# Eight modulation units between the layers, and the experts' outputs scattered in token order

## The chip, the core and the metric

The kernel runs on one core of a Trainium2 chip. The metric is the device time of one execution in microseconds (us). TensorE is called PE (its weight loads PEld), VectorE DVE, ScalarE ACT, GpSimd POOL and SyncE SP; a name with a q at its end (SPq, ACTq) is that engine's sequencer issuing a DMA.

## The reference

Two layers of a diffusion transformer block work on 256 context tokens and 256 x tokens of width 1024. All arithmetic is float32.

```python
mod = split(silu_c @ w_ada[l] + b_ada[l], 6)        # sh1, sc1, g1, sh2, sc2, g2; the same for ctx with silu_cc
hx = rms_norm(x, norm1_g[l]) * (1 + sc1) + sh1      # hc likewise
mix_x, mix_c = token_mixers(hx, hc, w_in[l], ...)   # differential, grouped and window attention
x = x + g1 * (mix_x @ w_out[l])
hx = rms_norm(x, norm2_g[l]) * (1 + sc2) + sh2
x = x + g2 * moe_ffn(hx, ...)                       # ctx too, except in the last layer
```

`moe_ffn` gives each token two of 16 experts (the best two of the best group of four); an expert computes `(silu(t @ w_gate) * (t @ w_up)) @ w_down` with 256 hidden columns, and the token's output is the sum of its two experts' outputs by their gates. The last layer updates x alone, and a final rms norm ends the program.

## The kernel before

Names in this section are those of the kernel's code; "layer one" is `l == 0`.

**Weights** pass through a ring of buffers (`Ring`), 1 MB each. `queue` writes down all loads of the program in the order in which they will be used. `load` takes the first of that list whenever a buffer is free, and issues its DMA on SP's queue; `take` hands the oldest loaded buffer to a user, `give` returns it and loads the next. Each buffer belongs to a pool that lives up to some layer (`last`). Pools are opened as SBUF comes free: `rawA` lives throughout, `rawB` opens ahead of the output projection, and `rawC` opens after it, ahead of the experts (two buffers in layer one, three in layer two). `upto` holds back loads of a later layer.

**Products** of float32 are made of three passes: ACT rounds a weight tile to a high part (`whi`, L234), DVE or POOL subtracts it to get the low part (`wlo`, L235), and `mm3` (L205 to L207) multiplies high by high, low by high and high by low.

**Modulation** of a layer is three thirds of `w_ada`, each eight loads (`kc`) of 1 MB. A unit (L459) multiplies one load with the two condition vectors in four groups of 32 columns of PE, into the PSUM bank `ada`. After the eighth unit of a third, DVE adds the bias (L465), PE transposes the row, and small products follow. `ada_third` is a generator that yields after each unit; `STEPS` says how many yields a third has. `fill(n)` runs n steps of it. `FILL` says for each layer how many steps run in the input projection, in attention and in the output projection: 28 in layer one's attention, 19 in layer two's, which are 16 units and three finishing steps. In attention these are spread over the items (L968 on): one tick of the loop works at several stages of several items in an order written by hand, and ends with the tick's share of `fill`. Each pool set of PSUM (`PS_IN`, `PS_ATT`, `PS_OUT`) has one of eight banks for `ada`; `PS_MOE` has none.

**Layer one's experts** (`experts`, L1006) work on 512 tokens, with 128 slots for each expert. `Route` picks the experts, and `lists` makes the list `idx` of the tokens of each expert, and `rows`, the place of each token's two outputs. Ahead of that the 512 normalized tokens were stored to `h2row` in DRAM, tile by tile, on SP's queue (L1772). POOL gathers an expert's tokens from there with an indirect DMA (L1025); PE transposes them (`tokens`), makes the hidden layer (`first`, `hidden`), and transposes it (`turn`); `second` multiplies with `w_down`. `write` copies the two PSUM banks of the output to `y` on ACT and issues a plain DMA of 128 rows on ACT's queue to `yrows` (L1095). `produce` splits the next weights: POOL makes the low part of the second half of `w_down`, DVE all others. The work of all engines is in the order written, since the loop is under a manual schedule. In the loop `write(n - 2)` follows `turn(n - 1)`, and two loads are let through in the last round.

**Between the layers** (`next_in`, L760) `combine` has POOL gather each token's two rows of `yrows` with eight indirect DMAs, by `rows`. For each of four tiles, `sum_pairs` makes the sum: ACT scales the first by its gate (`one`, L1405), DVE adds the second times its gate (`both`, L1408), `times` multiplies with g2 (L1411; on DVE for the first tile, on POOL for the other three), and DVE adds to x (L1414). Interleaved with it, `tokens_in` takes each tile through the norm (L655 makes `xn`), PE's transposes, the modulation and the high and low parts, and PE starts layer two's first block of `w_in` tile by tile. g2 comes broadcast into a buffer of the ring (`load_g2`).

**Layer two's experts** serve 256 tokens in pairs of experts (`expert_pairs`). They stream 48 MB of weights. They scatter their outputs into `prow` with an indirect DMA of POOL.

## Time and profile before

| what | value |
|---|---|
| time, median of 3 runs | 888.96 us (886.82 to 890.14) |
| the profiled execution | 888.22 us |
| its span in the profile | 886.3 us |
| PE busy | 784.3 us, 88% |
| DVE busy | 582.4 us, 66% |
| ACT busy | 447.6 us, 50% |
| POOL busy | 222.2 us, 25% |
| moved by DMA | 219.18 MB, mean 247 GB/s |

An engine's busy share is a mean over stages with different limits; which wait ends last in a stage is read from the stretches, the timelines and the chain of waits, whose rows stand below. In a timeline row the brackets hold the idle time ahead of the instruction and what ended it.

### The profile page before, as it was taken

What the parts mean: (1) busy time and instruction counts of PE and PEld (TensorE: products, weight loads), DVE (VectorE), ACT (ScalarE), POOL (GpSimd) and SP (SyncE); (2) the same over time, 40 slices, a digit from 0 to 9 for tenths busy, and PEclk for the clock granted to TensorE, in tenths of its full rate; (3) what the DMA queues carried; (4) which work ended last, traced back from release to release, by engine and by line L of the source; (5) the groups of instructions that cost most, each with busy time, mean ns of one, the idle gap of its engine ahead of it and who ended that gap; (6) DMA issues with size and microseconds to landing.
All of it is one profiled execution on the core that took longest, in us unless ns stands there. A gap on an engine that the chain in (4) does not pass through costs nothing.

```text
span 886.3 us, 12972 instructions
## 1 busy us (share of the span) xinstructions
PE 784.3 (88%) x4731; PEld 576.3 (65%) x4731; DVE 582.4 (66%) x1200; ACT 447.6 (50%) x861; POOL 222.2 (25%) x258
## 2 busy tenths in 40 slices
PE   4899999889989977999999549998899797999984
PEld 0578878445557746999999438887555565656541
DVE  1577673879863798899999586697667566221226
ACT  2454442667773416888888546462466543111112
POOL 2000101556320133443342472100423101000200
PEclk9999999999999988999999859999899997999987
DMA  9952221667879337899993757342188955999981
GB/s 319 344 185 96 95 96 48 247 270 284 275 214 376 121 148 263 306 388 401 400 408 156 249 195 292 128 158 95 51 331 215 340 186 215 350 423 422 419 333 51
DMA packets 54505, 219.18 MB, mean 247 GB/s; under 512 B 10299, under 2 KB 10299, under 8 KB 36640
## 3 DMA queue, kind: packets, MB, share of 16 engines
q1 hardware_dynamic: 40816, 182.34, 55.0%
q0 software_dynamic: 8736, 24.92, 7.9%
q10 hardware_dynamic: 4880, 11.00, 3.2%
q8 instruction: 39, 0.64, 0.3%
q14 instruction: 34, 0.28, 0.1%
HBM read 207.09 MB, written 16.84 MB: 253 GB/s over the span
## 4 chain that ended last, share of the span: by engine, by line
PE 66%; DVE 16%; DMA 8%; ACT 3%; issue 3%; POOL 2%; SPq 0%; ACTq 0%; POOLq 0%; DVEq 0%
PE mm L207 7%; PE mm L206 7%; PE mm L205 7%; PE tp L193 6%; PE gu L1189 6%; PE ada L459 4%; PE gu L207 4%; PE gu L205 3%; PE gu L206 3%; DMA wraw<-in_w_up 3%; PE sc L1466 3%; PE w L1245 3%; DVE wlo L235 2%; PE w L1154 2%; DVE nm L1480 2%
## 5 line engine op out<-in xcount | busy, mean ns | idle before, releaser
L235 DVE TENSOR_TENSOR wlo<-wraw,whi 128x1024 fp32r<-128x1024 f32 x136 | 186.1, 1392 | 43.0 <-ACT whi L234 40.5
L234 ACT CAST whi<-wraw 128x1024 fp32r<-128x1024 f32 x152 | 152.8, 1050 | 57.7 <-PE mm L207 35.5
L205 PE MATMUL mm<-whi,Xh 128*128 128x512 f32 x288 | 116.3, 405 | 5.1 <-ACT Xh L690 4.7
L206 PE MATMUL mm<-wlo,Xh 128*128 128x512 f32 x288 | 115.3, 400 | 0.5 <-DVE wlo L235 0.5
L207 PE MATMUL mm<-whi,Xl 128*128 128x512 f32 x288 | 115.0, 399 | 0.5 <-DVE Xl L694 0.5
L221 POOL TENSOR_TENSOR rstd<-ms,cst 128x1 f32<-128x1 f32 (+2 forms) x34 | 29.4, 864 | 272.1 <-DVE ms L219 263.2
L1493 ACT ACTIVATE e<-sc,nm 128x512 f32<-128x512 f32 (+1 forms) x96 | 58.4, 613 | 42.4 <-DVE nm L1486 22.6
L207 PE MATMUL gu<-whi,xl 128*128 128x256 f32 x256 | 74.3, 290 | 0.0
L205 PE MATMUL gu<-whi,xh 128*128 128x256 f32 x256 | 74.2, 290 | 0.0
L206 PE MATMUL gu<-wlo,xh 128*128 128x256 f32 x256 | 72.7, 284 | 0.0
L1189 PE MATMUL gu<-wraw,xq 128*64 128x256 f32 x512 | 64.4, 396 | 3.7 <-DMA wraw<-in_w_up 3.7
L205 PEld LDWEIGHTS mm<-whi,Xh 128*128 128x128 f32 x288 | 55.1, 191 | 18.7 <-ACT Xh L690 6.2
L207 PEld LDWEIGHTS mm<-whi,Xl 128*128 128x128 f32 x288 | 55.0, 191 | 13.9 <-DVE Xl L694 1.5
L206 PEld LDWEIGHTS mm<-wlo,Xh 128*128 128x128 f32 x288 | 55.1, 191 | 12.8 <-DVE wlo L235 1.2
L235 POOL TENSOR_TENSOR wlo<-wraw,whi 128x1024 fp32r<-128x1024 f32 x16 | 42.7, 2672 | 81.1 <-ACT whi L234 50.3
L1189 PEld LDWEIGHTS gu<-wraw,xq 128*64 128x64 f32 x512 | 37.9, 142 | 24.1 <-DMA wraw<-in_w_up 4.2
L193 PEld LDWEIGHTS tp<-ident,e 128*128 128x128 f32 x240 | 26.1, 142 | 40.8 <-issue 21.1
L1480 DVE TENSOR_REDUCE nm<-sc 128x1 f32<-128x512 f32 x64 | 41.2, 684 | 16.5 <-PE sc L1466 11.6
L207 PEld LDWEIGHTS gu<-whi,xl 128*128 128x128 f32 x256 | 49.3, 193 | 1.1 <-DVE xl L1050 0.4
L205 PEld LDWEIGHTS gu<-whi,xh 128*128 128x128 f32 x256 | 49.6, 194 | 0.3 <-ACT xh L1049 0.3
L206 PEld LDWEIGHTS gu<-wlo,xh 128*128 128x128 f32 x256 | 49.5, 193 | 0.0
L193 PE MATMUL tp<-ident,e 128*128 128x128 f32 x240 | 37.8, 286 | 8.4 <-DVE e L1534 3.9
(348 smaller groups left out, 1625.4 us busy)
## 6 DMA issues: line engine op xcount, KB each, us to landing
wraw<-in_w_ada SPq DMA_DIRECT2D x40, 1024.0 KB, 4.9
wraw<-in_w_gate SPq DMA_DIRECT2D x32, 1024.0 KB, 10.1
wraw<-in_w_up SPq DMA_DIRECT2D x32, 1024.0 KB, 11.0
wraw<-in_w_down SPq DMA_DIRECT2D x32, 1024.0 KB, 14.1
wraw<-in_w_in SPq DMA_DIRECT2D x14, 1024.0 KB, 5.2
wraw<-in_w_ada SPq DMA_DIRECT2D x16, 512.0 KB, 8.1
yrows<-y ACTq DMA_DIRECT2D x16, 512.0 KB, 8.1
wraw<-in_w_in POOLq DMA_DIRECT2D x5, 1024.0 KB, 11.9
```

The costliest lines, as they stand in the source:

```text
L193: self.nc.tensor.transpose(out, in_, self.k["ident"][:n, :n])
L205: mm(out, lhsT=xh, rhs=wh, start=start, stop=False)
L206: mm(out, lhsT=xh, rhs=wl, start=False, stop=False)
L207: mm(out, lhsT=xl, rhs=wh, start=False, stop=stop)
L221: nc.gpsimd.tensor_tensor(r, ms, self.k["mhalf"][:, :width], OP.pow)
L234: nc.scalar.copy(h, raw[:, lo:hi])
L235: (engine or nc.vector).tensor_tensor(l, raw[:, lo:hi], h.bitcast(F32), OP.subtract)
L459: nc.tensor.matmul(ps[32 * j:32 * j + 32, :], lhsT=self.silu_c[:, kc, :], rhs=raw[:, 512 * j:512 * j + 512], start=kc == 0, stop=kc == NKC ...
L1189: nc.tensor.matmul(gu[PSLOTS * g:PSLOTS * g + PSLOTS, 256 * b:256 * b + 256], lhsT=xq[q][:, kc, c:c + PSLOTS], rhs=raw[:, kc * 256:kc * 25 ...
L1245: nc.tensor.matmul(y[hf][gs], lhsT=hT[:, c, 0:PSLOTS] if p == NP else hT[:, c, gs], rhs=raw[:, c * D + o * 512:c * D + o * 512 + 512], sta ...
L1480: V.reduce_max(self.nm[:, i:i + 1], self.ps[i], axis=AX.X)
L1493: nc.scalar.activation(self.e[i][:, :self.nkey], self.ps[i], AF.Exp, scale=0.125, bias=self.nm[:, i:i + 1], accum_out=self.z[i])
```

## The change

- `ada` gets a PSUM pool of its own, one bank, open from the start until layer two's experts; the other sets lose their `ada` bank.
- Eight of layer two's units (`GAP`, third 1, 8 MB of `w_ada`) are queued after layer one's expert weights, the next g2 and half of the first block of `w_in`; they may use only buffers of pools that end with layer one. PE runs them after the last `write` of layer one's experts (`fill(GAP)`). Layer two's attention then has 13 steps, eight of them units; layer one's has 31 steps, its units as before. Each third has one step more, since the addition of the bias became a step of its own.
- Layer one's `rawC` has four buffers in place of two. A free buffer is chosen by the least `last`, and a loaded one is taken by its name.
- The experts' outputs of layer one go to `orow`, whose rows stand in the order (token, first or second pick): POOL scatters an expert's rows there with an indirect DMA by a list `outs`, which leaves unused slots out. `idx` is `outs` shifted right by one; `rows` is no longer computed. The last expert but one is written ahead of the last.
- `combine` loads with eight plain DMAs, four on SP's queue and four on ACT's. All four `times` are on DVE, and the order of the steps in `next_in` is changed.

```diff
     0, 128, 256, 512, 640, 768, 784, 788, 796, 804, 820, 821, 837, 839)
-RAW = dict(A=4, D=2, B=(4, 3), C=(2, 3))
+RAW = dict(A=4, D=2, B=(4, 3), C=(4, 3, 2))
 WSP = dict(proj=4, out=(4, 4), moe=5)
-PS_IN = dict(mm=4, ada=1, tp=3)
-PS_ATT = dict(sc=3, ada=1, tp=2, poA=1, poB=1)
-PS_OUT = dict(mm=2, tp=2, rps=1, pps=1, ips=1, ada=1)
+PS_IN = dict(mm=4, tp=3)
+PS_ATT = dict(sc=3, tp=2, poA=1, poB=1)
+PS_OUT = dict(mm=2, tp=2, rps=1, pps=1, ips=1)
...
 CBS = (4, 2, 1, 0, 3)
-FILL = ((0, 28, 0), (0, 19, 0))
+FILL = ((0, 31, 0), (0, 13, 0))
+GAP = 8
...
         self.upto = 2
-    def add(self, key, src):
-        self.todo.append((key, src))
+    def add(self, key, src, layer=None, fits=None):
+        layer = key[1] if layer is None else layer
+        self.todo.append((key, src, layer, fits or (lambda last: last >= key[1])))
...
         for _ in range(min(n or len(self.todo), len(self.todo))):
-            if not n and self.todo[0][0][1] > self.upto:
+            key, src, layer, fits = self.todo[0]
+            if not n and layer > self.upto:
                 break
-            slot = next((s for s in self.free if s[2] >= self.todo[0][0][1]), None)
+            slot = min((s for s in self.free if fits(s[2])), key=lambda s: s[2], default=None)
...
                 break
-            key, src = self.todo.popleft()
+            self.todo.popleft()
...
             self.load()
-        k, slot, t = self.live.popleft()
-        assert k == key, (k, key)
-        return t, slot
+        unit = next(u for u in self.live if u[0] == key)
+        self.live.remove(unit)
+        return unit[2], unit[1]
...
             self.h2row = self.dram.tile([512, D], F32, name="h2row")
-            self.yrows = self.dram.tile([NEXP * SLOTS * max(self.npass), D], F32, name="yrows")
+            self.orow = self.dram.tile([1024, D], F32, name="orow")
...
             self.queue()
+            adap = tc.tile_pool(name="adap", bufs=1, space=PSUM, reuse_waits="tile")
+            self.adap, self.close_adap = adap.__enter__(), lambda: adap.__exit__(None, None, None)
...
         steps = deque((l, third, kc) for l in range(2) for third in range(1 - l, 3) for kc in range(self.STEPS[third]))
-        def ada(n):
+        def ada(n, *where):
...
                     ring.add(("ada", l, third, kc), a["w_ada"][l].rearrange("(p k) n -> p k n", k=NKC)[
-                        :, kc, third * 2048:third * 2048 + 2048])
+                        :, kc, third * 2048:third * 2048 + 2048], *where)
...
                 ring.add(("ada0", 0, h, q), w[:, 2 * q:2 * q + 2, 0:2, h, :])
-        def block(name, l, cb, n):
-            for h in range(2):
+        def block(name, l, cb, n, halves=(0, 1), *where):
+            for h in halves:
...
                 else:
-                    ring.add((name, l, cb, h), src.rearrange("(k p) n -> p k n", p=128))
+                    ring.add((name, l, cb, h), src.rearrange("(k p) n -> p k n", p=128), *where)
...
             for i, cb in enumerate(CBS):
-                block("w_in", l, cb, fw[2 * i:2 * i + 2])
+                block("w_in", l, cb, fw[2 * i:2 * i + 2], (1,) if l and not i else (0, 1))
...
                         ring.add(("w_down", l, q, f), a["w_down"][l, f].rearrange("(p k) n -> p k n", k=2))
-            ring.add(("g2", l + 1), lambda t, l=l: self.load_g2(l, t))
+            ring.add(("g2", l + 1), lambda t, l=l: self.load_g2(l, t), l)
+            if l == 0:
+                block("w_in", 1, CBS[0], (0, 0), (0,), 0)
+                ada(GAP, 0, lambda last: last == 0)
...
             nc.gpsimd.dma_start(self.n1g, a["norm1_g"][0].rearrange("(k p) -> p k", p=128))
-        ps = self.bank("ada")
+        ps = self.adap.tile([128, 512], F32, tag="ada", name="ada")
...
             dma(g, a["norm1_g"][l].rearrange("(k p) -> p k", p=128))
-        ps = self.bank("ada")
+        ps = self.adap.tile([128, 512], F32, tag="ada", name="ada")
...
             self.ring.give(slot)
-            if kc < NKC - 1:
-                yield
+            yield
...
         yield
-    STEPS = (9, 10, 9)
+    STEPS = (10, 11, 10)
...
         rc_cm, rc = opened("rawC", "left")
-        self.ring.open(rc, "rawC", RAW["C"][paired], l)
+        self.ring.open(rc, "rawC", RAW["C"][0 if l == 0 else 1 if paired else 2], l)
...
         self.wsp, self.nwsp = mo, WSP["moe"]
+        if l == 1:
+            self.close_adap()
...
                 self.experts(l, mo, route[0])
-                self.gates, self.rows = route[1:]
+                self.gates = route[1]
...
                     self.chunk(ps, [t], kc, parts)
-            for name, t in (("one", 0), ("both", 0), ("times", 0), ("one", 1), ("add", 0)):
+            for name, t in (("one", 0), ("one", 1), ("both", 0), ("times", 0), ("add", 0)):
...
             step(ins, 0, "root")
-            step(sums, 1, "times", self.nc.gpsimd)
...
                 step(ins, t - 1, "scale")
-                step(sums, t + 1, "both")
-                step(sums, t + 1, "times", self.nc.gpsimd)
-                step(sums, t, "add")
+                step(sums, t, "times")
...
                 step(ins, t - 1, "high", 1)
+                step(sums, t, "add")
...
                 step(ins, t, "root")
+                step(ins, t - 1, "low", 1)
+                step(sums, t + 1, "both")
...
                     self.ring.until(2, self.nc.gpsimd)
-                step(ins, t - 1, "low", 1)
...
             return route
-        return route.lists(), route.gates, route.rows
+        return route.lists(), route.gates
...
                 out=xg[n % 3], out_offset=None, in_=self.h2row[:, :],
-                in_offset=bass.IndirectOffsetOnAxis(ap=lists[ps][:, e:e + 1], axis=0),
+                in_offset=bass.IndirectOffsetOnAxis(ap=lists[ps][0][:, e:e + 1], axis=0),
...
                 self.copy(y[:, hf * 512:hf * 512 + 512], ys[n][hf], True)
-            r0 = (e * self.npass[l] + ps) * SLOTS
-            self.written = nc.scalar.dma_start(self.yrows[r0:r0 + SLOTS, :], y)
+            self.written = nc.gpsimd.indirect_dma_start(
+                out=self.orow[:, :], out_offset=bass.IndirectOffsetOnAxis(ap=lists[ps][1][:, e:e + 1], axis=0),
+                in_=y, in_offset=None, bounds_check=2 * T * 128 - 1, oob_is_err=False)
...
                     turn(n - 1)
-                if n > 1:
+                if 1 < n < N:
...
                     tokens(n + 1)
-                if n == N - 1:
-                    ring.load(n=1)
...
                 if n == N - 1:
-                    ring.load(n=1)
+                    write(n - 1)
             write(N - 1)
+            if l == 0:
+                self.fill(GAP)
...
         self.pairs_of = {}
-        n = NEXP * SLOTS * self.npass[l]
-        for i, t in enumerate((0, 1, 2, 3) if l == 0 else (2, 3)):
-            y = [cb.tile([128, D], F32, tag="yc", name="yc", bufs=8) for _ in range(2)]
+        tiles = (0, 1, 2, 3) if l == 0 else (2, 3)
+        rows = self.orow[:, :].rearrange("(i p w) d -> i p w d", p=128, w=2)
+        for i, t in enumerate(tiles):
+            y = cb.tile([128, 2, D], F32, tag="yc", name="yc", bufs=4)
             for w in range(2):
-                self.nc.gpsimd.indirect_dma_start(
-                    out=y[w], out_offset=None, in_=self.yrows[:n, :],
-                    in_offset=bass.IndirectOffsetOnAxis(ap=self.rows[:, w, i:i + 1], axis=0),
-                    bounds_check=n - 1, oob_is_err=False)
-            self.pairs_of[t] = y, i
+                (self.nc.scalar if w else self.nc.sync).dma_start(y[:, w], rows[i, :, w])
+            self.pairs_of[t] = [y[:, w] for w in range(2)], i
...
         self.gates = m.rt.tile([128, 2, T], F32, tag="gates", name="gates")
-        self.rows = m.rt.tile([128, 2, T], I32, tag="rows", name="rows")
-        self.oh = tile_("oh", [2, T, 16])
+        self.oh = tile_("oh", [2, T, 16], F16)
...
                                    accum_out=self.pos[:, w, i:i + 1])
-        V.tensor_scalar(self.val[:, :, i], self.oh[:, :, i], cst[:, C_TOK + i:C_TOK + i + 1], None, OP.mult)
+        V.tensor_tensor(self.val[:, :, i], self.oh[:, :, i], cst[:, C_TOK + 2 * i:C_TOK + 2 * i + 2].unsqueeze(2)
+                        .broadcast_to([128, 2, 16]), OP.mult)
...
         m, V, T = self.m, self.nc.vector, self.T
-        lists, first = [], self.work.tile([128, 2, T], F32, name="first")
+        lists = []
...
             ips = self.ips
-            if ps == 0:
-                V.tensor_copy(first, self.pos)
-            else:
+            if ps:
...
                     self.picked(ips, i)
-            idx = m.rt.tile([128, 16], I32, tag=f"idx{ps}", name="idx")
-            V.tensor_scalar(idx, ips[:, 0:16], float(NONE), None, OP.add)
-            lists.append(idx)
+            idx, out = (m.rt.tile([128, 16], I32, tag=f"{n}{ps}", name=n) for n in ("idx", "outs"))
+            V.tensor_scalar(out, ips[:, 0:16], 2.0 * NONE, None, OP.add)
+            V.tensor_single_scalar(idx, out, 1, OP.logical_shift_right)
+            lists.append((idx, out))
...
             V.reduce_max(m.over[:, self.l:self.l + 1], self.pps[:, 64:80], axis=AX.X)
-        pick, e = self.small([2, T, 16], "picke"), self.small([2, T], "e")
-        V.tensor_tensor(pick, self.oh, self.k["cst"][:, C_EXP:C_EXP + 16].unsqueeze(1).unsqueeze(1).broadcast_to(
-            [128, 2, T, 16]), OP.mult)
-        V.reduce_sum(e, pick, axis=AX.X)
-        V.scalar_tensor_tensor(self.rows, e, float(SLOTS * m.npass[self.l]), first, OP.mult, OP.add)
```

## Rows read from the trace of the kernel before

In rows of stretches (start:end and length in us) a number in brackets is the count of instructions.

**Rows 1.** The chain that ended last, by line, the page's part 4 (shares of the span).

```profile
PE mm L207 7%; PE mm L206 7%; PE mm L205 7%; PE tp L193 6%; PE gu L1189 6%; PE ada L459 4%; PE gu L207 4%; PE gu L205 3%; PE gu L206 3%; DMA wraw<-in_w_up 3%; PE sc L1466 3%; PE w L1245 3%; DVE wlo L235 2%; PE w L1154 2%; DVE nm L1480 2%
```

**Rows 2.** Stretches in layer two's attention: PE, PEld, DVE, ACT, POOL, PEclk, DMA, GB/s.

```profile
639.00:660.00 21.00, 21.00 (x156) 12.89 (x155) 13.49 (x30) 14.13 (x35) 5.71 (x11) 1.00 0.90 335
...
660.00:676.00 16.00, 14.01 (x97) 8.72 (x98) 14.75 (x38) 10.17 (x26) 9.37 (x15) 1.00 0.61 226
...
676.00:689.00 13.00, 13.00 (x104) 7.03 (x100) 7.22 (x22) 9.41 (x25) 0.00 (x0) 1.00 1.06 231
```

**Rows 3.** PE's timeline in there: start, us, engine, line, operation, tile, count.

```profile
640.34 1.06 PE L459 MATMUL ada<-wraw,silu_c 128*32 128x512 f32 x8
...
641.33 1.09 PE L193 MATMUL tp<-ident,e 128*128 128x128 f32 x8
```

**Rows 4.** The same stretches, matmuls of `ada` alone: PE, PEld, PEclk, DMA, GB/s.

```profile
639.00:660.00 21.00, 7.04 (x56) 1.31 (x56) 1.00 0.90 335
...
660.00:676.00 16.00, 2.99 (x24) 0.57 (x24) 1.00 0.61 226
...
676.00:689.00 13.00, 4.80 (x40) 0.89 (x40) 1.00 1.06 231
```

**Rows 5.** PE's timeline after attention; in brackets the idle time before.

```profile
691.06 0.63 PE L193 MATMUL tp<-ident,modrow 128*128 128x128 f32 x4 [1.74 <-DVE modrow L467]
```

**Rows 6.** Two stretches ahead of and within layer two's experts.

```profile
740.00:750.00 10.00, 9.99 (x70) 8.14 (x69) 6.55 (x33) 3.54 (x5) 1.41 (x3) 0.83 0.04 14
...
770.00:780.00 10.00, 10.00 (x84) 6.49 (x84) 1.61 (x4) 1.89 (x4) 1.08 (x1) 1.00 1.00 404
```

**Rows 7.** PE's timeline between the layers.

```profile
520.51 1.97 PE L193 MATMUL tp<-ident,xn 128*128 128x128 f32 x8 [20.12 <-DVE xn L655]
```

**Rows 8.** Stretches at the end of layer one's experts.

```profile
474.00:488.00 14.00, 14.00 (x97) 12.72 (x96) 13.55 (x14) 12.34 (x19) 3.35 (x2) 1.00 0.12 48
...
488.00:502.00 14.00, 11.45 (x72) 9.90 (x70) 7.58 (x8) 7.75 (x12) 5.99 (x2) 1.00 0.63 225
```

**Rows 9.** Stretches at the start of layer one's experts.

```profile
323.00:330.00 7.00, 3.45 (x20) 2.10 (x20) 6.41 (x34) 1.57 (x4) 2.12 (x3) 0.78 0.99 373
...
332.00:334.00 2.00, 0.28 (x5) 0.18 (x4) 1.92 (x20) 0.00 (x0) 0.00 (x0) 0.50 0.63 262
```

**Rows 10.** SP's queue there.

```profile
331.35 0.33 SPq L1772 DMA_DIRECT2D h2row<-h  x1
```

**Rows 11.** POOL's timeline there.

```profile
335.75 1.14 POOL L1025 DMA_INDIRECT xg<-h2row,idx  x1 [5.99 <-DVE gates L1867]
```

**Rows 12.** The steady stretch of layer one's experts.

```profile
360.00:487.30 127.30, 127.30 (x916) 119.10 (x915) 119.85 (x117) 112.48 (x157) 50.02 (x23) 1.00 0.89 350
```

**Rows 13.** POOL and ACT's queue within it.

```profile
442.84 2.64 POOL L235 TENSOR_TENSOR wlo<-wraw,whi 128x1024 fp32r<-128x1024 f32 x1 [5.14 <-issue]
...
440.27 0.33 ACTq L1095 DMA_DIRECT2D yrows<-y  x1
...
450.01 0.33 ACTq L1095 DMA_DIRECT2D yrows<-y  x1
```

**Rows 14.** DMA issues of layer two's scatters: count, median us from issue to landing.

```profile
prow<-yr,prows POOLq DMA_INDIRECT x6, 8.9
```

**Rows 15.** The chain between the layers: start, us, what.

```profile
501.05 2.96 DMA yrows<-y
```

**Rows 16.** ACT's and DVE's timelines between the layers.

```profile
504.11 1.99 ACT L234 CAST whi<-wraw 128x1024 fp32r<-128x1024 f32 x2 [3.08 <-DMA yrows<-y]
...
511.76 1.28 DVE L1408 SCALAR_TENSOR_TENSOR yc<-yc,gates 128x1024 f32<-128x1024 f32 x1 [0.79 <-DMA yc<-yrows,rows]
...
513.08 1.23 DVE L1411 TENSOR_TENSOR yc<-yc,wraw 128x1024 f32<-128x1024 f32 x1
...
517.62 2.83 DVE L655 TENSOR_SCALAR xn<-xc,rstd 128x1024 f32<-128x1024 f32 x1 [0.69 <-POOL rstd L221]
```

**Rows 17.** Durations of a line on POOL: least/median/most ns, first and last start.

```profile
L1411 POOL TENSOR_TENSOR yc<-yc,wraw x3: 2332/2442/3277, 517.6 to 531.1; 128x1024 f32<-128x1024 f32 x3
```

More of the change, by code (lines that the diff above doesn't have):

```diff
@@ L96, in shape_constants @@
     k[:, C_GW:C_GW + 4] = np.array([4, 3, 2, 1], np.float32)
-    k[:, C_TOK:C_TOK + 8] = np.tile(np.arange(4)[None, :] * 128 + i - NONE, 2)
+    k[:, C_TOK:C_TOK + 8] = 2 * (np.arange(8)[None, :] // 2 * 128 + i) + np.arange(8)[None, :] % 2 - 2 * NONE
     k[:, C_MH:C_EXP] = -0.5
@@ L1916, in extra @@
         V.tensor_scalar(eid, eid, 15.0, float(16 * self.l), OP.min, OP.add)
-        idf = small(1, "idf")
+        idf = small(1, "px")
         V.scalar_tensor_tensor(idf, eid, 128.0, cst[:, C_ROW:C_ROW + 1], OP.mult, OP.add)
```

## The prediction

> **What bounds the kernel now.** I read first the page's chain of waits by line, to see which engine carries the end: of the modulation work `ada` alone is 4% of it, next to the three-pass products, so units taken off PE there are worth looking for [rows 1]. Second, the stretches of layer two's attention, where eight of those units go away: PE is busy 48.0 of 50 us (21.0, 14.0 and 13.0), DVE 35.5, ACT 33.7; PE decides [rows 2]. Third, PE's own lines with its records of `ada` by stretch, for the price of a unit [rows 3, 4]. Then SP's issues and the stretches where layer one's experts begin, POOL's rows in their steady state, and all engines between the layers, because the change touches queues there.
>
> **Attention of layer two.** One unit is a row of eight matmul records; what follows it on PE starts 0.99 us later (640.34 to 641.33) [rows 3]. Sixteen units ran here, 7 of them in the first of the three stretches, 3 in the second and 5 in the third (56, 24 and 40 records) [rows 4]. Eight go: 8 × 0.99 = −7.9. With them goes the wait at the end of the third, where PE stood 1.74 us for the modulation row on DVE [rows 5]: the add that makes this row is now a step of its own, a tick of attention ahead of PE's transposes. PE without the units would still be busy 48.0 − 7.9 = 40.1 us, above DVE's 35.5. But in the second stretch DVE is already ahead of PE (14.75 to 14.0 us) [rows 2], so the half of its 3 units gives nothing: +1.5; and I add 1.1 for ticks elsewhere in which DVE or ACT will end last. I take −7.9 − 1.7 + 1.5 + 1.1 = −7.0. Ends: −9.6 (the two gains alone) and −3.9 (no tail, 13 of 16 units outside the second stretch count, 6.4, less 2.5 for DVE and ACT). The gain travels to the end if what comes next moves with it. At 740 to 750, before layer two's experts, the DMA is idle, 4%, because the ring of weight buffers is full; from 770 it is full [rows 6]: that stream starts when buffers come free, thus earlier by the same time. One to one.
>
> **Where the eight units go.** They run after layer one's last expert, where PE's first product of layer two waited 20.12 us, until 520.5 [rows 7]: 8 × 0.99 = 7.9 us fit, if their 8 MB have landed. In 474 to 502 us the DMA moved 48 and 225 GB/s, 3.8 MB in all [rows 8]. The new loads (`g2` 1 MB, `w_in` 1 MB, 8 MB of units) find buffers from about 475 us, as the last experts give them back; at the 373 GB/s of another full stretch [rows 9] 10 MB take 27 us, so the last lands at 502 and PE ends at about 509, before 520. Cost: nothing; without the cover it would be 7.9 less than before, that is, the attention's gain given back.
>
> **Start of layer one's experts.** `rawC` has four buffers instead of two, so SP issues 2 MB more at about 323 us, ahead of the last `h2row` store, which it issued at 331.35 [rows 10]. The two loads and a store filled the DMA until 330 (99%, 373 GB/s), and the last store ran alone in 332 to 334 [rows 9]. 2 MB more at 373 GB/s are 5.4 us: the DMA is busy until 335.4 and the store lands at about 337 instead of 333.5. The first token gather started at 335.75, when the lists had come from DVE [rows 11]; it would start at 337 + 0.8, +2.2 us. Ends: 0 (the store is served beside the loads) and +3.2 (the gather also queues behind the remaining data). I take +2.0. The Trainium skill ("DMA: Bandwidth & Descriptors", "Queues, rings and completion order") says that each DMA engine takes one queue's work in order and turns between queues packet by packet; store and loads share SP's queue, so by the page the whole of the 2 MB precedes the store, and the sum would have +3.2 here. The rows show loads and store only one after the other, which agrees but doesn't prove it.
>
> **Steady state of the experts.** PE is busy throughout 360 to 487 us [rows 12]. The plain write leaves ACT (0.33 us of issue) and an indirect one, 1.14 us by a gather of the same size [rows 11], comes to POOL, which idled 5.14 us before its low half at 442.84; the y that it would scatter was ready at about 440.27, when ACT issued the write [rows 13]. It fits with some 1.5 us to spare: 0, unless the scatters wait for one another (second rival). Of the rows only the valid half is written: 0.25 MB less an expert, on a DMA that isn't full (350 GB/s) [rows 12]: 0. `lists` loses the row computation and gains a shift: +0.1.
>
> **Between the layers.** Before, the last plain write of y was issued at 501.05 and landed 2.96 us later [rows 15]; ACT's first split of `w_in` waited for that landing (its buffer was y's) and began at 504.11 [rows 16]. Now the last scatter starts at about 501.1 on POOL. No scatter of this size in a quiet DMA is in the trace; below it stands the plain write's 2.96, above it the 8.9 us of layer two's six scatters, made under full load [rows 14, 15]. I take 5.5, nearer to the plain one, since the DMA is emptying: landing at 506.6, +2.6 against 504.0 (0 to +6). Then ACT has four splits of 1.0 us ahead of the loads of the second outputs on its queue, 0.33 of issue and about 2.96 for the landing: the first `both` at 506.6 + 0.1 + 4.0 + 0.33 + 2.96 = 514.0 instead of 511.76: +2.2 [rows 15, 16]. After it the path is shorter: POOL no longer multiplies (2.3 to 3.3 us each) while DVE works; DVE's `xn` took 2.83 us beside one such product, and DVE's own multiply of the same size 1.23: −1.6 [rows 16, 17]. In return DVE has three multiplies more, 3 × 1.23 = 3.7 us, of which I let 2.0 delay the third and fourth tile, the rest lies in DVE's waits for PE. Sum +2.6. Ends: −1 (landing as before, multiplies hidden) and +6 (landing at 510).
>
> The eight gathers on POOL become plain loads on SP and ACT; both move 4 MB, and only the first pair is awaited: 0.
>
> **Layer one's attention** runs the same units in other places: 0 ± 1.
>
> **Sum:** −7.0 + 2.0 + 2.6 + 0.1 = −2.3. Against the profiled execution, 888.2 us (span 886.3, 1.9 around it), that is 885.9. It lies 0.7 below the median of the three runs, so by the median 886.7.
>
> **Rivals.**
> First, the DMA costs stay out: the store passes the loads, the scatter lands in 3 to 4 us. Then −7.0 + 0 − 0.5 = −7.5: 881.5. For it: the stretch of the store shows an otherwise idle DMA, and the DMA is emptying at 502 [rows 8, 9]. Against: splits stand ahead of the loads on ACT.
> Second, slower: scatters chained through `orow`. All sixteen write one tensor at rows known only on the chip, so scatter n may wait on POOL for n − 1 to land; behind it there wait POOL's low half and the next gather, and PE waits for both. It decides once a landing exceeds one expert's 9.74 us (440.27 to 450.01) [rows 13]: what it exceeds adds up from expert to expert, and beyond POOL's spare 1.5 us it is PE's. Six scatters in layer two landed at a median of 8.9 [rows 14]: near enough that a full DMA passes it. At 10.5 us, 0.75 over on each of 14 experts, less 1.5: +9.0, so 886.7 + 9.0 = 895.7. Against: this DMA is at 89%, not full [rows 12], and half of the rows are dropped. The Trainium skill (same page, "Two DMAs through the same engine are not ordered") states that a DMA that depends on another's bytes must wait for its completion semaphore; the page doesn't say whether such a wait is made here, and if it is, this is the price.
> Third, attention doesn't follow PE: DVE and ACT take over within the ticks and −3.9 is all: −3.9 + 4.7 = +0.8, 889.8. For it: DVE is the busiest of the second stretch [rows 2]. Against: PE had no gap in two of the three stretches [rows 2].
>
> **How the numbers follow.** Forecast 0.50 (own range 882 to 892); first rival 0.25; second 0.15; third 0.10. Within 0.5%, 4.4 us, a measurement of this kernel can't tell from no change: 884.5 to 893.4. Of the forecast's 0.50 I put 0.12 below that and 0.04 above. Faster 0.25 + 0.12 = 0.37; slower 0.15 + 0.04 = 0.19; same 0.44. Range 878 to 896: the half of the second rival and a little of the first lie outside.
>
> **What would show it.** Right: in layer two's attention 8 units fewer and PE still the busiest, its stretch 5 to 8 us shorter; PE's first experts' product 1 to 3 us later after `lists`; the eight units on PE between 501 and 510; the first `both` 2 us later after the last copy. Wrong: POOL waiting for a scatter in the midst of the experts; PE waiting for `wraw` in the gap beyond 520; a DVE `modrow` that ends last in the ticks.

## The result: slower by 0.8%, and the profile after

| | before | changed |
|---|---|---|
| median of 9 runs each | 888.64 us (885.55 to 891.10) | 894.97 us (893.02 to 899.25) |
| ratio | | 1.008, 95% interval 1.0056 to 1.0104 |
| profiled execution, span | 888.22, 886.3 us | 893.10, 890.8 us |

The first record of each stage on PE (on DVE for the first `both`, the sum of a token's two outputs) cuts both profiled spans into the same stretches; "last product" stands for the last row of products of its kind. The last column is the forecast, the one before it the measured difference.

| stretch | before | changed | difference | forecast |
|---|---|---|---|---|
| start to layer one's attention | 154.63 | 155.27 | +0.6 | 0 |
| to its first product of `w_out` | 111.79 | 113.10 | +1.3 | 0 ± 1 |
| to the first product of the experts | 75.16 | 76.43 | +1.3 | +2.1 |
| to the last product of y | 158.43 | 158.73 | +0.3 | 0 |
| to the first `both` | 11.75 | 19.58 | **+7.8** | +2.2 |
| to the first transpose of layer two | 8.75 | 6.79 | −2.0 | −1.6 |
| to layer two's attention | 105.38 | 106.80 | +1.4 | +2.0 |
| to its last product | 71.35 | 64.03 | **−7.3** | −7.0 |
| to the end | 189.06 | 190.07 | +1.0 | 0 |
| sum | 886.3 | 890.8 | +4.5 | −2.3 |

Each column is one execution. The pair holds 4.5 of the 6.3 us between the medians; where the rest lies, no profile here shows. Stretches vary between profiles even where the code is the same: layer one's attention took 110.7 to 114.7 us in eight kernels that have the same steps there, and the last stretch 186.0 to 190.1 us in all fourteen profiles of this document. So what counts are the two large rows. The attention came out as forecast: sixteen units to eight, 7.3 us. Its first and last rows on PE, before and changed:

```profile
625.89 1.32 PE L1466 MATMUL sc<-kT,qhl 128*128 128x512 f32 x5
697.24 1.08 PE L1640 MATMUL poB<-ptB,vBC 128*64 128x256 f32 x8
```

```profile
636.70 1.32 PE L1477 MATMUL sc<-kT,qhl 128*128 128x512 f32 x5
700.73 1.95 PE L1651 MATMUL poB<-ptB,vBC 128*64 128x256 f32 x16
```

All of it, and 0.5 more, went into the time from the last product of y to the first `both`. First the timelines of POOL, SP, ACT, DVE and PE there in the changed kernel (start, us, instruction; in brackets the idle time before and what ended it), put together by engine:

```profile
493.17 1.88 POOL L1106 DMA_INDIRECT orow<-y,outs  x1 [4.99 <-ACT y L216]
504.37 0.98 POOL L1106 DMA_INDIRECT orow<-y,outs  x1 [3.12 <-ACT y L216]
513.43 0.96 POOL L1106 DMA_INDIRECT orow<-y,outs  x1 [8.08 <-issue]
...
481.12 17.16 SPq L161 DMA_DIRECT2D wraw<-in_w_ada  x7
...
503.27 1.28 ACT L216 COPY y<-y 128x512 f32<-128x512 f32 x2 [2.44 <-PE y L212]
517.18 1.04 ACT L239 CAST whi<-wraw 128x1024 fp32r<-128x1024 f32 x1 [12.63 <-DMA orow<-y,outs]
...
523.11 1.28 DVE L1419 SCALAR_TENSOR_TENSOR yc<-yc,gates 128x1024 f32<-128x1024 f32 x1 [0.22 <-DMA yc<-orow]
...
503.85 5.63 PE L471 MATMUL ada<-wraw,silu_c 128*32 128x512 f32 x48
511.94 1.94 PE L471 MATMUL ada<-wraw,silu_c 128*32 128x512 f32 x8 [2.46 <-DMA wraw<-in_w_ada]
514.56 1.94 PE L471 MATMUL ada<-wraw,silu_c 128*32 128x512 f32 x8 [0.68 <-DMA wraw<-in_w_ada]
529.90 1.97 PE L198 MATMUL tp<-ident,xn 128*128 128x128 f32 x8 [13.40 <-DVE xn L668]
```

Then the stretches (PE, PEld, DVE, ACT, POOL, PEclk, DMA, GB/s):

```profile
480.00:490.00 10.00, 10.00 (x73) 9.30 (x72) 10.00 (x10) 8.85 (x14) 4.20 (x2) 1.00 1.00 350
490.00:500.00 10.00, 10.00 (x69) 9.17 (x67) 9.35 (x10) 7.11 (x11) 6.80 (x3) 1.00 1.02 419
500.00:510.00 10.00, 8.70 (x62) 3.46 (x60) 0.42 (x1) 2.00 (x4) 2.23 (x2) 1.00 1.01 418
510.00:515.00 5.00, 2.37 (x12) 0.41 (x16) 0.00 (x0) 0.00 (x0) 1.50 (x2) 0.63 0.27 111
```

SP issues the loads of units from 481 us, and from then to 510 the DMA is full, where it had moved 48 and 225 GB/s [rows 8]. PE runs six units at once at 503.85 and waits for the last two until 514.56. The last y is copied by 504.55. Its scatter is issued at 513.43 only: POOL sat idle for 8.1 us after it had issued the scatter of the expert before, at 504.37, and went on when that one had had time to land. ACT's split waits for the last output to land, that is, for its data to be in memory; it begins at 517.18; before, 504.11 [rows 16]. The last plain write had landed 2.96 us after its issue [rows 15]; here ACT's split begins 12.6 us after the copy of the last output. From that split to the first `both` the changed kernel is 1.7 us faster than before (5.9 us instead of 7.7).

### The profile page after: what moved, and what is told of

The parts are those of the page before. It is cut to its first block, busy times and chain, and to the rows that moved or that the text cites. A ratio compares the mean times of both kernels' runs of the same rounds, so it can differ in the third digit from the quotient of the medians.

```text
span 890.8 us, 12983 instructions
## 1 busy us (share of the span) xinstructions
PE 789.9 (89%) x4731; PEld 578.6 (65%) x4731; DVE 588.4 (66%) x1200; ACT 447.1 (50%) x861; POOL 229.3 (26%) x263
## 5 line engine op out<-in xcount | busy, mean ns | idle before, releaser
L240 DVE TENSOR_TENSOR wlo<-wraw,whi 128x1024 fp32r<-128x1024 f32 x136 | 192.1, 1443 | 46.2 <-ACT whi L239 46.1
L1491 DVE TENSOR_REDUCE nm<-sc 128x1 f32<-128x512 f32 x64 | 41.5, 684 | 15.5 <-PE sc L1477 10.9
L471 PE MATMUL ada<-wraw,silu_c 128*32 128x512 f32 x320 | 43.6, 636 | 3.2 <-DMA wraw<-in_w_ada 3.1
```

Of the source, the lines that this page charges most:

```text
L240: (engine or nc.vector).tensor_tensor(l, raw[:, lo:hi], h.bitcast(F32), OP.subtract)
L471: nc.tensor.matmul(ps[32 * j:32 * j + 32, :], lhsT=self.silu_c[:, kc, :], rhs=raw[:, 512 * j:512 * j + 512], start=kc == 0, stop=kc == NKC ...
L1491: V.reduce_max(self.nm[:, i:i + 1], self.ps[i], axis=AX.X)
```

## Experiments

The theory after the comparison: the loads of the moved units fill the DMA until after the last outputs, and everything that the sums wait for lands late. The chain of the scatters, my rival before, was taken to be a part of it. Rivals: the chain alone, the scatter as an operation, the new order of `next_in`.

**Plain writes again, eight units kept.**

```diff
-            self.written = nc.gpsimd.indirect_dma_start(out=self.orow[:, :], ...)
+            self.written = nc.scalar.dma_start(self.yrows[r0:r0 + SLOTS, :], y)
-                (self.nc.scalar if w else self.nc.sync).dma_start(y[:, w], rows[i, :, w])
+                self.nc.gpsimd.indirect_dma_start(out=y[:, w], ..., in_=self.yrows[:n, :], ...)
```

> The changed kernel, with the experts' outputs written as before (plain writes on ACT's queue into yrows, eight gathers by rows on POOL); the eight units between the layers, four rawC buffers and the order of next_in stay. Theory (the scatters wait for one another through orow, 493.2, 504.4 and 513.4 us, because the eight loads of units fill the DMA from 480 to 510): without the chain the last write is issued at 504.6 and lands by about 511 instead of 517.1; the first 'both' some 4 us earlier than 523.1, total 889 to 891. Rival A (the loads of the units alone make the last landing late, chained or not): the write lands after 515 and the total stays at 894 or more. Rival B (the new order of next_in with all multiplies on DVE is what costs): also 894 or more, with the time lost behind the first 'both'.

Measured: 890.86 us, ratio to before 1.0018 (1.0002 to 1.0034). Its timeline on ACT, the last write and the split that waits for it:

```profile
503.99 0.33 ACTq L1107 DMA_DIRECT2D yrows<-y  x1
...
511.59 1.99 ACT L239 CAST whi<-wraw 128x1024 fp32r<-128x1024 f32 x2 [7.63 <-DMA yrows<-y]
```

The same plain write that landed in 2.96 us before needs 7.6 us. From the last product of y to the first `both` it is 17.2 us: 5.4 more than before, without any scatter, and 2.4 less than changed. The time came out as the theory said, but the larger part of the loss is here without a chain. PE's units by themselves hold up nothing here: POOL's first gather for the sums starts 0.9 us behind the split (512.48), as before (504.95, behind 504.11).

**No units between the layers, scatters kept.**

```diff
-FILL = ((0, 31, 0), (0, 13, 0))
+FILL = ((0, 31, 0), (0, 21, 0))
-GAP = 8
+GAP = 0
```

> The changed kernel with GAP = 0: the eight units go back into layer two's attention (21 steps there), so the DMA is quiet at the end of layer one's experts; the scatters stay. Theory: the scatters land in about 4 us each although they are chained, the last at 508 to 509, the first 'both' at about 515, some 8 us earlier; attention of layer two gets 7.3 us longer again: total 893 to 896, about that of the changed kernel. Rival A (units' loads alone delay the landing) expects the same here and differs in the run with plain writes. Rival C (an indirect scatter lands late by itself, whatever else the DMA does): the last landing stays 8 us or more after its start, first 'both' no more than 2 us earlier, total 900 or more.

Measured: 891.62 us, ratio 1.0041 (1.0021 to 1.0061), 1.4 us below the expected range. POOL's last two scatters and ACT's split behind them:

```profile
502.56 0.98 POOL L1106 DMA_INDIRECT orow<-y,outs  x1 [0.15 <-issue]
506.52 0.97 POOL L1106 DMA_INDIRECT orow<-y,outs  x1 [2.98 <-ACT y L216]
...
509.88 1.05 ACT L239 CAST whi<-wraw 128x1024 fp32r<-128x1024 f32 x1 [4.22 <-DMA orow<-y,outs]
```

In a quiet DMA the scatter lands in 3.4 us and the chain costs less than 1 us (the last y is copied at 505.66). The first `both` comes after 11.1 us, earlier than before. That excludes the scatter as an operation, and the order of `next_in`, which is the changed one here, as causes of the late `both`. It does not make them free: without any unit moved, this kernel is 3 us slower than the kernel before. Which of the other parts (lists, scatters, buffers, order, steps) costs that, no run takes apart.

**Two output tensors in turn**, so that a scatter waits for the last but one. The sums take the first pick from one tensor and the second from the other, so the results are not the reference's. Both are set to zero ahead, at the start of the program in one run and in layer one's output projection in the other (the diff leaves this out):

```diff
+            self.orow2 = self.dram.tile([1024, D], F32, name="orow2")
-                out=self.orow[:, :], out_offset=...
+                out=(self.orow2 if n % 2 else self.orow)[:, :], out_offset=...
```

> The changed kernel with two tensors for the outputs, odd experts scatter into the second, so that a scatter waits only for the last but one; both are set to zero at the start of the program (8 MB of writes in the input projection, where the DMA is at 22%), and the sums take the first pick from one and the second from the other, so they are not the reference's. Theory: the last two scatters start within 5 us of each other at about 500.7 and 504.6, the last lands by 512 instead of 517.1, and the first 'both' comes 4 to 5 us earlier than 523.1: total 890 to 891. Rival A (only the full DMA counts): landing after 515, total 894 or more.

> The changed kernel with two output tensors in turn, as in the run before, but their 8 MB of zeros are written in the output projection of layer one, where the DMA is at 13% from 300 us, so that the start of the program is untouched; the sums are not the reference's. Theory (the chain adds to the flood): scatter 15 starts as soon as its y is copied, lands 9 us later in the full DMA; from the last product of y to the first 'both' about 16 us instead of 19.6, total 891 to 892. Rival A (the flood alone): 19 us or more, 894 to 896.

The first, 919.5 us, says little: its zeros delayed the first weights by 27 us. The second took 894.56 us, ratio 1.0088 (1.0065 to 1.0111), as the changed kernel.

```profile
503.55 0.98 POOL L1117 DMA_INDIRECT orow<-y,outs  x1 [0.15 <-DMA orow<-y,outs]
506.93 0.96 POOL L1117 DMA_INDIRECT orow<-y,outs  x1 [2.40 <-ACT y L216]
...
516.02 1.04 ACT L239 CAST whi<-wraw 128x1024 fp32r<-128x1024 f32 x1 [9.37 <-DMA orow<-y,outs]
```

The last scatter starts at 506.93, as soon as its y is copied, and lands 9.1 us later: it no longer waits for the one before it, and the first `both` comes after 18.6 us instead of 19.6. So the theory's part on the chain failed (16 us expected) and rival A holds: with all eight loads in flight the wait costs nearly the same on POOL as in the DMA. Counted from the last product of y, the split that waits for the landing came 3.3 us earlier than in the changed kernel, but from ACT's first load for the sums to the first `both` it then took 7.9 us (from 516.36) instead of 5.7 (from 517.46). The last unit ran 1.3 us later here, so I estimate the chain's own share at 1 to 2 us.

**Half of the units**, with scatters and with plain writes, and **two buffers fewer with all eight**:

```diff
-GAP = 8
+GAP = 4
-FILL = ((0, 31, 0), (0, 13, 0))
+FILL = ((0, 31, 0), (0, 17, 0))
...
-RAW = dict(A=4, D=2, B=(4, 3), C=(4, 3, 2))
+RAW = dict(A=4, D=2, B=(4, 3), C=(2, 3, 2))
```

> The changed kernel with four units between the layers instead of eight (GAP 4, 17 steps in layer two's attention). Theory (the loads of the units keep the DMA full until after the last scatter, and its landing waits for them): 4 MB less end the full stretch at about 500, so scatter 14 and 15 land in 3 to 5 us each; from the last product of y to the first 'both' 11 to 13 us instead of 19.6, and layer two's attention 66 to 68 us, against 64.0 with eight and 69.2 with none: total 886 to 889. Rival (what is lost between the layers is in proportion to the units, whenever their loads end): about 15.5 us to the first 'both', total 892 to 894.

> The run with plain writes with four units between the layers instead of eight. Theory: the plain write lands in about 3 us in a DMA that is no longer full, first 'both' 11 to 13 us after the last product of y instead of 17.2: total 885 to 888. Rival (in proportion): 14.5 us, total 889 to 891.

> The changed kernel with two rawC buffers in layer one, as before. If the additional loads delay the first token gather (its landing 5.4 us instead of 4.4), from the first product of the output projection to the first of the experts takes 75.2 to 75.5 us instead of 76.4: -1. The prediction's reason (the last h2row store waits behind 2 MB of loads) would give -2 or more there. Against both: with two buffers fewer the units' loads begin later and their full stretch ends later, so the first 'both' could come up to 3 us later. Total 892 to 896.

| | units, rawC | last unit on PE | first `both` | attention two | time, ratio to before |
|---|---|---|---|---|---|
| no units, scatters | 0, 4 | | 11.1 | 69.2 | 891.62, 1.0041 |
| half, scatters | 4, 4 | all at 0.3 | 13.8 | 66.7 | 890.70, 1.0028 (1.0011 to 1.0045) |
| half, plain | 4, 4 | all at 0.3 | 12.0 | 66.8 | 886.92, 0.9982 (0.9969 to 0.9994) |
| plain | 8, 4 | 9.4 | 17.2 | 65.6 | 890.86, 1.0018 |
| changed | 8, 4 | 11.0 | 19.6 | 64.0 | 894.97, 1.008 |
| eight, two buffers fewer | 8, 2 | 21.7 | 25.5 | 65.5 | 901.63, 1.0145 (1.0127 to 1.0163) |

The columns in between are us after the last product of y. What decides is when the last load of a unit has come, and neither their number nor the scatter by itself: four units with plain writes cost 0.3 us to the first `both`, eight cost 5.4, and eight loaded later, with scatters, cost 13.8. In the kernel with two buffers fewer PE waits for the load of each unit from the second on, and the time lies 5.6 us above the expected range; these are the third and the last:

```profile
513.45 1.42 PE L471 MATMUL ada<-wraw,silu_c 128*32 128x512 f32 x8 [3.34 <-DMA wraw<-in_w_ada]
...
528.29 1.93 PE L471 MATMUL ada<-wraw,silu_c 128*32 128x512 f32 x8 [0.55 <-DMA wraw<-in_w_ada]
```

The rival "in proportion" is refuted by plain writes (12.0, not 14.5). ACT's last write and the split behind it in that run:

```profile
507.02 0.33 ACTq L1107 DMA_DIRECT2D yrows<-y  x1
...
509.99 1.99 ACT L239 CAST whi<-wraw 128x1024 fp32r<-128x1024 f32 x2 [3.00 <-DMA yrows<-y]
```

With scatters the theory was too low: 13.8 us, above its 11 to 13 and below the rival's 15.5, because the last scatter still waited 3 us for the one before it:

```profile
507.08 0.98 POOL L1106 DMA_INDIRECT orow<-y,outs  x1 [2.87 <-ACT y L216]
511.05 0.96 POOL L1106 DMA_INDIRECT orow<-y,outs  x1 [2.98 <-issue]
```

Its total of 886 to 889 was missed as well: the profile has 6.5 us more than before already at the last product of y, which the units don't explain.

**The additional steps alone**, on the kernel before, and **the changed kernel without those of layer one**:

```diff
-FILL = ((0, 28, 0), (0, 19, 0))
+FILL = ((0, 31, 0), (0, 21, 0))
-            if kc < NKC - 1:
-                yield
+            yield
```

> The kernel before with one part of the change alone: the addition of the bias is a step of its own (31 and 21 steps in the attentions), no units between the layers, outputs and buffers as before. Theory (of the 7.3 us that layer two's attention gained, some 2 are the wait for the modulation row, which goes with this alone, as in the run without units, 69.2 against 71.4): total 886 to 887. Rival (all of the gain is the eight units): no change, 888.4.

> The changed kernel with the 28 steps of before in layer one's attention (the bias's addition is a step of its own in layer two's thirds 1 and 2 alone). Theory (with 31 steps PE waits 1.95 us ahead of a transpose of the modulation row and its clock falls to 0.83 behind it): layer one's attention 111.8 us instead of 113 to 115, total 892 to 893. Rival (variation between programs): no change, 894 to 895.

The first: 887.78 us, ratio 0.9992 (0.9979 to 1.0005), no change; the gain that the theory expected is not in the time. In its profile layer two's attention takes 69.3 us instead of 71.4, as expected, and layer one's 114.6 instead of 111.8. (The profiled execution took 890.09 us, the slowest of its kernel, so the 114.6 is at the upper end.) PE's transpose of the modulation row there, in the kernel before, in the changed one and in this one:

```profile
243.99 0.63 PE L193 MATMUL tp<-ident,modrow 128*128 128x128 f32 x4 [0.96 <-ACT se L1496]
```

```profile
244.68 0.70 PE L198 MATMUL tp<-ident,modrow 128*128 128x128 f32 x4 [1.95 <-ACT se L1507]
```

```profile
246.00 0.78 PE L193 MATMUL tp<-ident,modrow 128*128 128x128 f32 x4 [1.95 <-ACT se L1495]
```

In all eight kernels with 31 steps whose start is undisturbed, PE waits 1.93 to 1.96 us for ACT here, in the five with 28 steps 0.94 to 0.96. In seven of the eight the granted clock is 0.83 in one of the two stretches of 10 us behind it, in one of the five with 28. The eight take 113.4 us on average (110.7 to 114.7), the five 111.7 (110.5 to 112.3). The longer wait goes with the 31 steps in every profile; the lower clock does not: the fastest of the eight, 110.7 us, has the same wait and a granted clock of 1.00 throughout. So of the 1.7 us between the averages 1.0 is the longer wait at most, and the rest can be the variation of single executions.

The second run refuted its own total: attention takes 110.5 us as the theory said, but the time is 897.25 us, ratio 1.0102 (1.0075 to 1.013). Its experts start later: the first transposes of gathered tokens came 8.5 us after the gather's start (4.4 before, 5.4 changed), and PE's output projection took 1.5 us longer than in the changed kernel. That the loads for the four `rawC` buffers fell upon the gather is likely by two of the runs below, but not shown in this kernel; why the output projection was longer stays open.

**What the runs point to:** the move of units alone, with four of them and 28 steps in layer one; outputs, lists and `next_in` as before.

```diff
+GAP = 4
-FILL = ((0, 28, 0), (0, 19, 0))
+FILL = ((0, 28, 0), (0, 17, 0))
-            if kc < NKC - 1:
+            if kc < NKC - 1 or l and third:
                 yield
```

> The kernel before with the part of the change that moves units, and nothing else: the PSUM pool, the ring, four rawC buffers, four units between the layers, and the step of its own for the bias in layer two's attention alone (28 steps in layer one's, as before; 17 in layer two's). Plain writes, lists, gathers and the order of next_in as before. Theory (the flood of loads and the additional steps in layer one's attention are what the change pays): layer one's attention 111.8 us, the last product of y to the first 'both' 12 us, layer two's attention 66.8 instead of 71.4: 884 to 885, 4 less than before. Rival (the steps of layer one cost nothing; the 113 to 115 us of the runs so far are a variation between programs): as the run with plain writes and four units, 886.5 to 887.5.

Measured: 885.49 us, ratio 0.9967 (0.9949 to 0.9985), 0.5 us above the expected range and below the rival's. Left over is 2.2 us at the start of the experts, where the first transposes come 6.3 us after the gather's start. So two more, with three `rawC` buffers, and with two buffers and two units:

> The faster version (four units between the layers, nothing else of the change) with three rawC buffers in layer one instead of four. Theory: the additional loads at 330 to 340 us are what makes the first token gather land 6.3 us after its start instead of 4.4, so half of that comes back (-1); in return the last unit's load ends some 3 us later, which is still before the last write of y lands (11.6 to 13 us to the first 'both'): total 884 to 886. Rival (two buffers fewer cost with four units what they cost with eight, 6 us per two): 888.

> The faster version with two units between the layers and the two rawC buffers of before. Theory: the first gather lands after 4.4 us as before (-1.9 against the version with four), the first 'both' 11.6 to 12.5 us after the last product of y, layer two's attention 68.0 to 68.5 instead of 66.8 (+1.4): total 884.5 to 886. Rival (the landing of the gather has nothing to do with the rawC loads): 887.

Three buffers: 883.38 us, ratio 0.9951 (0.9932 to 0.9969), faster than both kernels. Two and two: 887.56 us, ratio 0.9991 (0.9971 to 1.0012), no change. The first transposes follow the gather's start by 4.5 and 4.3 us, as before, so the fourth buffer's load is what hit them. With two buffers PE gets the second unit only 5.7 us after the last product of y, the split behind the last write waits 6.0 us, and the first `both` comes after 14.5 us; layer two's attention takes 69.3 us. Both miss what was expected (11.6 to 12.5, 68.0 to 68.5): even two units cost if their loads end late. The profile of the version with three, POOL's gather, ACT's last write and split, the units on PE, and the stretch:

```profile
336.03 1.14 POOL L1039 DMA_INDIRECT xg<-h2row,idx  x1 [5.99 <-DVE gates L1881]
...
501.75 0.33 ACTq L1109 DMA_DIRECT2D yrows<-y  x1
504.77 1.99 ACT L239 CAST whi<-wraw 128x1024 fp32r<-128x1024 f32 x2 [3.05 <-DMA yrows<-y]
...
501.03 3.64 PE L471 MATMUL ada<-wraw,silu_c 128*32 128x512 f32 x32
...
490.00:500.00 10.00, 8.78 (x55) 7.70 (x54) 6.06 (x6) 5.63 (x8) 7.73 (x5) 1.00 0.50 199
```

All four units run in one piece, the write lands in 3.0 us as before, and the DMA is at half in the ten us ahead of it. All other stretches are within 0.3 us of before but layer two's attention, 66.9 us instead of 71.4, and that to the end, 1.0 us shorter, which is within that stretch's variation.

## Why the prediction was wrong

**The step that failed** is "Where the eight units go", with its "Cost: nothing", and behind it "I take 5.5, nearer to the plain one, since the DMA is emptying". Both sentences look at the same 30 us and contradict each other. I counted 10 MB of loads into the stretch that ends at 502 and asked whether PE would be done before 520; it was, at 516.5, and that is all that I asked. The count itself was early: SP issued the units' loads from 481, not 475, and PE got the last one at 514.5. The landing of the outputs I then took as if the DMA were the one of before. The upper end, 8.9 us from layer two's scatters under full load, was the one that applied to a single landing, and its condition was in my own sum: the moved loads are the full load. With the wait of the last scatter for the one before it, the changed kernel went beyond that end: landing at about 517, not 510. The plain write's 7.6 us and the scatter's 9.1 us in that DMA are the term's real size, against 2.96 and 3.4 in a quiet one. The term of +2.2 measured +7.8: ACT's split began 9.6 us later behind its copy than before, less the 1.7 us gained from there to the first `both`.

**Rivals.** The second rival had the right sign and nearly the total (895.7), for a reason that holds only in part: the scatters do wait for one another, but in the midst of the experts POOL's next scatter came 9.7 us later and never too late (that stretch +0.3 us). The wait decides at the last scatters alone, and taking it away gained nothing in time; the rival priced it at 9.0 us where it cost 1 to 2, so its total is luck. The first rival (the DMA costs stay out) and the third are refuted.

**What held.** The attention: −7.0 forecast, −7.3 measured, of which about 2 come from the step of its own alone (71.4 to 69.3) and, by the kernels with scatters, 2.4 from the first four units and 2.7 from the other four (1.2 by those with plain writes, 66.8 to 65.6). The gain is not lost later on: from there to the end it is +1.0, within that stretch's variation. The sums: −1.6 and +2.0 for the multiplies on DVE, −2.0 and +1.4 measured. The +1.4 is the favourable end: in the nine kernels with the new order of `next_in` that stretch took 106.8 to 109.5 us, in the five with the old one 105.1 to 106.3, so in most of them the new order won nothing on balance. The steady state of the experts: 0 and +0.3.

**Right only in its size.** The start of the experts was to lose 2.0 us because the last `h2row` store waits behind 2 MB of loads. (Its sum, 337 + 0.8 against 335.75, is +2.05 and not the +2.2 that stands there.) It lost 1.3, but not for that. SP's queue in the changed kernel shows the store ahead of the additional loads:

```profile
333.30 0.33 SPq L1782 DMA_DIRECT2D h2row<-h  x1
333.68 0.42 SPq L161 DMA_DIRECT2D wraw<-in_w_down  x1
334.19 0.74 SPq L161 DMA_DIRECT2D wraw<-in_w_gate  x1
```

The rule of the Trainium skill that the prediction named, on the order in a queue, was thus never put to the test. With two `rawC` buffers the same 76.4 us were measured, so in the changed kernel it isn't the loads either. The work on DVE that makes the gather's list takes 0.35 us longer (from its `ohs` to the gather 1.78 us before, 2.13 changed, where the prediction had +0.1), and the gather's issue takes POOL 2.15 us instead of 1.14 [rows 11]. In the version with plain writes, four units and four buffers the loads do cost there: 6.3 us from the gather's start to the transposes, against 4.5 with three buffers.

**Missed.** Layer one's attention was taken as "the same units in other places". With three steps more PE waits 1.0 us longer there; the averages of single profiles differ by 1.7 us, but no run shows that as time: the steps alone left it unchanged, and the changed kernel without them was no faster. The last 1.0 us, at the end of the program, is within that stretch's variation.

## What to carry to other kernels

Work that is moved into an engine's gap brings its loads along, and these use the time ahead of the gap: ask what lands there and who waits for it, and price that landing in the DMA as it will be, with the moved loads in it. How many units a gap takes is decided by the moment at which the last load ends, not by the gap's length on PE; here four of eight kept 4.5 of the 7.3 us, some 2 of them the step's own, and the first `both` came 0.1 us later than before. A generator with one step more is a new order everywhere it runs: look for what it wins in one stage and loses in another.

## What the runs showed of the hardware

The length of a gather's issue on POOL went with what DVE had begun. In the changed kernel POOL issued the first gather while DVE's subtraction of two 128x1024 inputs started beside it:

```profile
338.01 2.15 POOL L1037 DMA_INDIRECT xg<-h2row,idx  x1 [6.05 <-DVE gates L1874]
...
337.93 4.63 DVE L240 TENSOR_TENSOR wlo<-wraw,whi 128x1024 fp32r<-128x1024 f32 x4 [0.23 <-ACT whi L239]
```

In the kernel before that subtraction began 0.7 us after the gather (336.47), and the issue took 1.14 us. Of the fourteen kernels, the first gather's issue took 2.14 to 2.15 us in the seven where DVE began 0.1 us ahead of it, and 1.14 to 1.15 in the seven where DVE began 0.5 to 0.7 us behind it. These are also the kernels without and with the row computation in `lists`, and no run changed the moment alone, so it is an association. It isn't a fixed price: before, the second gather, issued at 338.15 in the midst of such subtractions, took 1.55 us. The Trainium skill ("GPSIMD Engine Reference", "1. Specifications") says that POOL shares its SBUF interfaces with DVE and contends with DVE's instructions that have two SBUF inputs; the rows on the first gather agree with it.
